# Rotary queries: four quarter-height ScalarE copies in place of a split and two permutation matmuls

## The chip, the cores and the metric

One core of a Trainium2 chip runs the whole program. The metric is the device time of one execution in microseconds (us); the times shown are of three executions of the kernel before.

## The reference, cut to what matters

The program is a two-layer decoder trunk over 1024 tokens of width 1024: an mLSTM layer, then a layer of latent attention, each with an MLP. The change lies in the attention layer's queries. Each of 8 heads has 128 plain and 64 rotary columns; the rotary ones are turned by the token's position:

```
def apply_rope(x, cos, sin):
    xf = x.astype(jnp.float32)
    x1, x2 = jnp.split(xf, 2, axis=-1)
    out = jnp.concatenate([x1 * cos - x2 * sin, x2 * cos + x1 * sin], axis=-1)
    return out.astype(x.dtype)
...
q = (cq @ w_q_b).reshape(B_, S, B_HEADS, B_NOPE + B_ROPE)
q_nope, q_rope = jnp.split(q, [B_NOPE], axis=-1)
q_rope = apply_rope(q_rope, cos[:, :, None, :], sin[:, :, None, :])
```

So a rotary query is x times cosines plus x with its two halves of 32 columns exchanged, times signed sines.

## The kernel before, in words

Activations lie transposed: features on the 128 partitions, 512 tokens (one half of the sequence) along the free axis. A float32 product is made of three TensorE matmuls: each operand is split into a rounded part hi (ScalarE copy, L499) and the rest lo (VectorE subtraction, L500), and `mm3` issues hi·hi, hi·lo and lo·hi (L280 to L282). Weights are split the same way after their DMA (L238 on ScalarE, L239 on VectorE).

The rotary queries of two heads (a "pair") fill one tile of 128 partitions: two heads times two halves of 32. Exchanging the halves therefore means that partitions 0-31 and 32-63 change places, and 64-95 and 96-127. This happens in `rope`, which is called for 4 pairs in each of the two halves of the sequence, 8 times in all. `rope` is a generator: the part ahead of its `yield` runs right behind the pair's matmuls, the part behind it some steps later. For the first half `rot` in `attention_first` calls it, for the second `prepare_pair` in `attention_second`; both hand the result to `query_rotary`, which splits it and writes the tile that the score matmuls read (L1762 on ScalarE, L1764 to L1767 on VectorE). I number the eight calls pair 1 to pair 8 in order of time.

The input of `rope`, `pt`, is a PSUM bank of the pool `pc` (two banks, shared with value projections, query projections and transposes of the softmax). The pools `ps` (two banks) and `pm` (two double banks) hold the dense work. `rope` takes tiles of the pool `tmc` (six).

Around it runs the dense work of an MLP: `two_streams` weaves the attention's steps with MLP steps, so that TensorE has matmuls of the MLP while the attention's vector work runs. Within that, a list scheduler with a timeline model of its own puts the instructions of each engine in an order when the program is built; a change of one step can so move others. Each engine runs its own list in order, and a wait holds all that stands behind it.

Names in the rows: `hd` is an MLP hidden tile (or a transposed softmax tile), `wk`, `wh`, `wl` are weights, `k` is a general 1024-column buffer, `tma` an accumulator of the adaLN vectors, `selW` the tile that holds the permutations. L980, L981 and L499 make a hidden tile's nonlinearity and its hi part on ScalarE, L500 on VectorE its lo part.

## Time and profile before

| | |
|---|---|
| time, median of 3 | 2322.63 us (2320.99 to 2323.7) |
| the profiled execution's own time | 2324.03 us |
| its span, first to last instruction | 2322.2 us |
| TensorE matmul busy | 2280.8 us (98%), 12042 matmuls |
| TensorE weight loads busy | 1921.8 us (83%) |
| VectorE busy | 1702.5 us (73%) |
| ScalarE busy | 1129.4 us (49%) |
| mean granted clock of TensorE | 0.998 |

Rows of a timeline give the start (us from the span's start), the duration, the engine, the line, the operation, output<-inputs and, in brackets, idle time ahead of it and who ended it. PE is TensorE's matmuls, DVE VectorE, ACT ScalarE. Matmuls and vector instructions overlap their successor's start, so the step from one start to the next is the price in a full queue, not the duration.

### The profile page before, as it was taken

How to read it: one execution, taken by the hardware profiler on the slowest of the kernel's cores; microseconds unless marked ns; L12 is line 12 of the kernel's file. 1: busy time of each engine (PE TensorE's matmuls, PEld its weight loads, DVE VectorE, ACT ScalarE, POOL GpSimd, SP SyncE). 2: the span in 40 equal slices, each digit the busy share in tenths (PEclk: the TensorE clock that was granted, in tenths of full speed). 3: DMA queues.
4: the chain of work that ended last, by engine and by line, in shares of the span. 5: the costliest groups of instructions: out<-in, count | busy, mean ns of one | idle time of the engine just before them, and what ended most of it. 6: DMA issues, size and time to landing. Idle time of an engine off the chain costs nothing.

```text
span 2322.2 us, 32704 instructions
## 1 busy us (share of the span) xinstructions
PE 2280.8 (98%) x12042; PEld 1921.8 (83%) x12042; DVE 1702.5 (73%) x2782; ACT 1129.4 (49%) x1919; POOL 90.7 (4%) x196
## 2 busy tenths in 40 slices
PE   8999999999999999999999999999999999999998
PEld 6888788888887877778888788888888888989997
DVE  6676776889887877677775687666666388788776
ACT  4364435765334445545444565434444454655443
POOL 1000000001022210000000000000000000000000
PEclk9999999999999999999999999999999999999999
DMA  9543454667999887666785654774334352445432
GB/s 320 173 129 118 134 176 153 196 220 267 330 276 295 277 283 275 191 192 203 238 256 186 226 199 145 252 236 151 129 99 149 115 168 82 146 149 173 128 109 109
DMA packets 401649, 444.38 MB, mean 191 GB/s; under 512 B 27123, under 2 KB 289328, under 8 KB 401488
## 3 DMA queue, kind: packets, MB, share of 16 engines
q1 hardware_dynamic: 388544, 397.09, 54.0%
q0 software_dynamic: 12944, 45.20, 5.2%
q8 instruction: 95, 1.56, 0.3%
q14 instruction: 66, 0.54, 0.1%
HBM read 343.65 MB, written 98.57 MB: 190 GB/s over the span
## 4 chain that ended last, share of the span: by engine, by line
PE 78%; DMA 8%; DVE 8%; issue 2%; ACT 2%; SPq 1%; POOL 0%; DVEq 0%; ACTq 0%; POOLq 0%
PE ps L280 13%; PE ps L282 13%; PE ps L281 13%; PE pm L280 8%; PE pm L281 8%; PE pm L282 8%; DMA raw<-in_mlp_w_dram 4%; PE pc L281 2%; PE pc L280 2%; PE pc L282 2%; DVE wl L239 1%; DVE k L247 1%; PE pc L1982 1%; DMA raw<-s 1%; PE pm L1787 1%
## 5 line engine op out<-in xcount | busy, mean ns | idle before, releaser
L238 ACT CAST wh<-raw 128x1024 fp32r<-128x1024 f32 (+2 forms) x317 | 321.4, 1016 | 430.5 <-PE ps L281 178.0
L239 DVE TENSOR_TENSOR wl<-raw,wh 128x1024 fp32r<-128x1024 f32 (+2 forms) x317 | 375.0, 1185 | 197.4 <-ACT wh L238 172.8
L280 PE MATMUL ps<-k,wh 128*128 128x512 f32 (+1 forms) x1252 | 476.4, 380 | 8.1 <-DVE u L247 1.6
L282 PE MATMUL ps<-k,wl 128*128 128x512 f32 (+1 forms) x1252 | 469.4, 375 | 0.5 <-DVE wl L239 0.5
L281 PE MATMUL ps<-k,wh 128*128 128x512 f32 (+1 forms) x1252 | 468.4, 374 | 0.0
L280 PEld LDWEIGHTS ps<-k,wh 128*128 128x128 f32 x1252 | 236.6, 189 | 55.0 <-issue 2.7
L282 PEld LDWEIGHTS ps<-k,wl 128*128 128x128 f32 x1252 | 236.3, 189 | 43.3 <-DVE wl L239 1.0
L281 PEld LDWEIGHTS ps<-k,wh 128*128 128x128 f32 x1252 | 236.6, 189 | 41.4 <-issue 1.4
L247 DVE TENSOR_TENSOR k<-k,pm 128x512 f32<-128x512 f32 (+1 forms) x250 | 192.3, 800 | 63.8 <-PE pm L282 63.2
L280 PE MATMUL pm<-wh,hd 128*128 128x512 f32 x488 | 193.5, 397 | 3.1 <-ACT raw L1793 1.8
L282 PE MATMUL pm<-wh,hd 128*128 128x512 f32 x488 | 190.5, 390 | 0.0
L281 PE MATMUL pm<-wl,hd 128*128 128x512 f32 x488 | 190.5, 390 | 0.0
L280 PEld LDWEIGHTS pm<-wh,hd 128*128 128x128 f32 x488 | 91.7, 188 | 24.8 <-ACT raw L1793 4.5
L282 PEld LDWEIGHTS pm<-wh,hd 128*128 128x128 f32 x488 | 91.7, 188 | 19.8 <-DVE hd L500 0.5
L281 PEld LDWEIGHTS pm<-wl,hd 128*128 128x128 f32 x488 | 91.8, 188 | 18.3 <-issue 0.5
L390 DVE SCALAR_TENSOR_TENSOR tma<-raw,cond,tma 128x512 f32<-128x512 f32 x120 | 89.5, 746 | 17.6 <-DMA raw<-in_ada_w_dram 8.4
L281 PE MATMUL pm<-hd,wk 128*128 128x512 f32 x256 | 100.1, 391 | 1.7 <-DVE hd L500 1.7
L1793 ACT ACTIVATE raw<-pm,sm 128x128 f32<-128x128 f32 (+3 forms) x64 | 47.5, 742 | 111.2 <-DVE sm L1792 107.6
L280 PE MATMUL pm<-hd,wk 128*128 128x512 f32 x256 | 100.9, 394 | 0.6 <-ACT hd L499 0.6
L280 PE MATMUL pm<-hd,wh 128*128 128x512 f32 x256 | 99.5, 390 | 1.1 <-ACT hd L499 0.8
L282 PE MATMUL pm<-hd,wl 128*128 128x512 f32 x256 | 99.9, 390 | 0.2 <-DVE wl L239 0.2
L281 PE MATMUL pm<-hd,wh 128*128 128x512 f32 x256 | 99.7, 390 | 0.2 <-DVE hd L500 0.2
(498 smaller groups left out, 4847.9 us busy)
## 6 DMA issues: line engine op xcount, KB each, us to landing
raw<-in_mlp_w_dram SPq DMA_DIRECT2D x176, 512.0 KB, 4.5
raw<-in_ada_w_dram SPq DMA_DIRECT2D x64, 512.0 KB, 4.6
raw<-in_mlp_w_dram SPq DMA_DIRECT2D x128, 256.0 KB, 4.7
raw<-in_a_w_in_dram SPq DMA_DIRECT2D x44, 512.0 KB, 4.3
lo<-wl POOLq DMA_DIRECT2D x32, 512.0 KB, 6.1
wk<-lo SPq DMA_DIRECT2D x64, 256.0 KB, 4.1
xs<-k SPq DMA_DIRECT2D x40, 256.0 KB, 4.5
raw<-in_a_w_out_dram SPq DMA_DIRECT2D x16, 512.0 KB, 4.8
```

What stands on the lines that cost most here:

```text
L238: nc.scalar.copy(hi[:, :n], r[:, :n])
L239: i = nc.vector.tensor_sub(lo[:, :n], r[:, :n], hi[:, :n].bitcast(F32))
L247: return f(*a, **k)
L280: nc.tensor.matmul(o, lh, rh, start=start, stop=False)
L281: nc.tensor.matmul(o, lh, rl, start=False, stop=False)
L282: pe_last[0] = nc.tensor.matmul(o, ll, rh, start=False, stop=stop)
L390: nc.vector.scalar_tensor_tensor(acc, r[kk], cond[:, k : k + 1], acc, ALU.mult, ALU.add)
L1787: nc.tensor.matmul(o[:, :w], qh, kh, start=False, stop=True)
L1793: nc.scalar.activation(pr[:, :n], f, AF.Exp, bias=m, scale=SCALE, accum_out=l)
L1982: nc.tensor.transpose(pt[:, ts(2 * e + i, P)], u.prs[i][:, ts(b + e, P)], ident)
```

## The change

`rope` no longer splits `pt` and no longer multiplies by a permutation. Four ScalarE copies of 32 partitions each read `pt` in PSUM and write the exchanged quarters to an SBUF tile; VectorE multiplies that tile by the sines in place. The permutation in `selW` is not built any more. The two other uses of the permutation idea (`both`, `both_perm`, for the key) stay.

```
-    perm = selW[:, 0]
...
-            nc.vector.tensor_copy(perm[:, s], ident[:, ts(q ^ 1, 32)])
...
     def rope(pt, hf):
 
-        hi, lo, t1 = tmc(F32R), tmc(F32R), tmc()
-        split_mod(hi, lo, pt, None)
+        t1, t2 = tmc(), tmc()
+        for q in range(4):
+            nc.scalar.copy(t2[ts(q, 32)], pt[ts(q ^ 1, 32)])
         nc.vector.tensor_mul(t1, pt, hf.cs[:, 0])
         yield
-        p2 = pc()
-        nc.tensor.matmul(p2, perm, lo, start=True, stop=False)
-        nc.tensor.matmul(p2, perm, hi, start=False, stop=True)
-        t2 = tmc()
-        nc.vector.tensor_mul(t2, p2, hf.cs[:, 1])
+        nc.vector.tensor_mul(t2, t2, hf.cs[:, 1])
         nc.vector.tensor_add(t1, t1, t2)
         return t1
```

In the changed program the copies are L1530, the two products L1531 and L1533 and the sum L1534 (before: L1532, L1538, L1539). Lines behind `rope` stand 5 lower: `query_rotary` is L1757 and L1759 to L1762, softmax L1786 to L1790.

The scheduler moves the rest. First place: VectorE around pair 2. Before (`tmc_9431` is pair 2's lo part, `tmc_9432` its product with the cosines, `hd_9450` the hidden tile):

```order
L239 TENSOR_TENSOR wl_9417<-raw_9413,wh_9416 128x640 [waits DMAHW5_49,DMAHW6_49,PE_49,Activation_49]
L1795 TENSOR_SCALAR raw_9385<-raw_9385,sm_9407 128x256 [waits DVE_49]
L247 TENSOR_TENSOR tmc_9124<-tmc_9124,ps_9436 128x512 [waits PE_49]
L500 TENSOR_TENSOR hd_9450<-tmc_9124,hd_9450 128x512 [waits Activation_49]
L366 TENSOR_REDUCE sm_9494<-pc_9489 128x4 [waits PE_49]
```

The same place now (`tmc_9424` is what the copies write, `hd_9444` the same hidden tile):

```order
L239 TENSOR_TENSOR wl_9410<-raw_9406,wh_9409 128x640 [waits DMAHW5_49,DMAHW6_49,PE_49,Activation_49]
L1531 TENSOR_TENSOR tmc_9423<-pc_9413,hd_8492 128x512 [waits Activation_49]
L1533 TENSOR_TENSOR tmc_9424<-tmc_9424,hd_8492 128x512
L247 TENSOR_TENSOR tmc_9117<-tmc_9117,ps_9430 128x512 [waits PE_49]
L1534 TENSOR_TENSOR tmc_9423<-tmc_9423,tmc_9424 128x512 [waits DVE_49]
L1759 COPY k_1650_9503<-tmp_9504 64x512 [waits Activation_49]
L1760 COPY k_1650_9503<-tmp_9504 64x512
L1761 TENSOR_TENSOR k_1650_9503<-tmc_9423,tmp_9504 64x512 [waits DVE_49]
L1762 TENSOR_TENSOR k_1650_9503<-tmc_9423,tmp_9504 64x512
L500 TENSOR_TENSOR hd_9444<-tmc_9117,hd_9444 128x512 [waits Activation_49]
L366 TENSOR_REDUCE sm_9488<-pc_9483 128x4 [waits PE_49]
```

The whole rest of `rope` and `query_rotary`, which stood behind the permutation matmuls, now stands ahead of the lo part of the hidden tile. The first product, L1531, waits for ScalarE, whose four copies read the same bank.

ScalarE at the same place now; before, one copy `tmc<-pc` of 128x512 stood first:

```order
L1530 COPY tmc_9424<-pc_9413 32x512 [waits PE_49]
L238 COPY wh_9409<-raw_9406 128x640 [waits DMAHW6_49,DMAHW5_49]
L1530 COPY tmc_9424<-pc_9413 32x512 x3
L1211 COPY wk_9450<-raw_9449 128x1024 [waits DMAHW7_49,DMAHW0_49,PE_49]
L980 ACTIVATE tmc_9117<-tmc_9117 128x512 [waits DVE_49]
L1757 COPY tmp_9504<-tmc_9423 128x512 [waits DVE_49]
L981 ACTIVATE tmc_9117<-tmc_9117 128x512 [waits Activation_49]
L499 COPY hd_9444<-tmc_9117 128x512 [waits Activation_49]
```

Three of the four copies stand behind a weight cast, and the first copy of `query_rotary` (L1757) has moved ahead of the hidden tile's last two steps.

Second place: TensorE at pair 2, where the hidden tile is read. Before:

```order
L364 MATMUL pc_9489<-ident,tma_9167 128x128 x4
L280 MATMUL pm_9463<-hd_9450,wk_9206 128x512
L281 MATMUL pm_9463<-hd_9450,wk_9206 128x512
L282 MATMUL pm_9463<-hd_9450,wk_9207 128x512
...
L1535 MATMUL pc_9507<-tmc_9431,selW 128x512
L1536 MATMUL pc_9507<-tmc_9430,selW 128x512
L280 MATMUL ps_9520<-hd_9368,k_1529_8851 128x256
```

Now:

```order
L364 MATMUL pc_9483<-ident,tma_9160 128x128 x4
L280 MATMUL pm_9457<-hd_9444,wk_9199 128x512
L281 MATMUL pm_9457<-hd_9444,wk_9199 128x512
L282 MATMUL pm_9457<-hd_9444,wk_9200 128x512
...
L280 MATMUL ps_9510<-hd_9361,k_1529_8847 128x256
```

The two matmuls with `selW` are gone; the readers of the hidden tile stand where they stood.

Third place: VectorE behind pair 3, at the keys of the next head (`k_1782` before, `k_1773` now). Before:

```order
L1539 TENSOR_TENSOR tmc_9995<-tmc_9995,tmc_10057 128x512 [waits DVE_49]
L500 TENSOR_TENSOR hd_10041<-u_1702_9747,hd_10041 128x512 [waits Activation_49]
L390 TENSOR_SCALAR tma_9912<-raw_10046,cond,tma_9912 128x512 [waits DMAHW0_49]
L500 TENSOR_TENSOR hd_10084<-pc_10085,hd_10083 128x512 [waits Activation_49]
L1764 COPY k_1766_10060<-tmp_10061 64x512 [waits Activation_49]
L1765 COPY k_1766_10060<-tmp_10061 64x512
L1766 TENSOR_TENSOR k_1766_10060<-tmc_9995,tmp_10061 64x512 [waits DVE_49]
L1767 TENSOR_TENSOR k_1766_10060<-tmc_9995,tmp_10061 64x512
L1791 TENSOR_REDUCE sm_10106<-pm_10092 128x1 [waits PE_49]
L390 TENSOR_SCALAR tma_9912<-raw_10046,cond,tma_9912 128x512 [waits DVE_49]
L500 TENSOR_TENSOR k_1782_10128<-ps_10130,k_1782_10128 128x512 [waits Activation_49]
```

Now:

```order
L1759 COPY k_1757_10047<-tmp_10048 64x512 [waits Activation_49]
L1760 COPY k_1757_10047<-tmp_10048 64x512
L1761 TENSOR_TENSOR k_1757_10047<-tmc_9983,tmp_10048 64x512 [waits DVE_49]
L1762 TENSOR_TENSOR k_1757_10047<-tmc_9983,tmp_10048 64x512
L1786 TENSOR_REDUCE sm_10093<-pm_10079 128x1 [waits PE_49]
L500 TENSOR_TENSOR hd_10032<-u_1696_9737,hd_10032 128x512 [waits Activation_49]
L390 TENSOR_SCALAR tma_9902<-raw_10037,cond,tma_9902 128x512 [waits DMAHW0_49]
L500 TENSOR_TENSOR hd_10071<-pc_10072,hd_10070 128x512 [waits Activation_49]
L1787 TENSOR_SCALAR sm_10093<-sm_10093 128x1 [waits DVE_49]
L500 TENSOR_TENSOR k_1773_10115<-ps_10117,k_1773_10115 128x512 [waits Activation_49]
```

`query_rotary` has moved from behind two other subtractions (`hd`) to ahead of them; between its end and the keys' subtraction stand other instructions than before.

## The prediction

> **What bounds the kernel now.** I read the page first: engine shares, the granted clock, the chain that ended last.

> ```profile
> PE 2280.8 (98%) x12042; PEld 1921.8 (83%) x12042; DVE 1702.5 (73%) x2782; ACT 1129.4 (49%) x1919; POOL 90.7 (4%) x196
> PEclk9999999999999999999999999999999999999999
> PE 78%; DMA 8%; DVE 8%; issue 2%; ACT 2%; SPq 1%; POOL 0%; DVEq 0%; ACTq 0%; POOLq 0%
> ```

> TensorE is busy for 98% of the span at full clock and holds most of the chain. Busy time alone does not say that its queue is full, since matmuls overlap. So I looked at the steps from one start to the next, in a timeline at the first of the eight places, and at its busy time by stretches around later ones.

> ```profile
> 978.49 0.39 PE L1535 MATMUL pc<-tmc,selW 128*128 128x512 f32 x1
> 978.72 0.39 PE L1536 MATMUL pc<-tmc,selW 128*128 128x512 f32 x1
> 978.95 0.39 PE L280 MATMUL pm<-hd,wk 128*128 128x512 f32 x1
> ```

> ```profile
> 1440.00:1460.00 20.00, 20.00 (x97) 16.89 (x97) 15.24 (x24) 8.28 (x13) 0.00 (x0) 1.00 0.86 288
> 1460.00:1480.00 20.00, 20.00 (x101) 16.98 (x100) 15.80 (x24) 9.26 (x16) 0.00 (x0) 1.00 0.77 241
> ```

> A 512-column matmul lasts 0.39 us but the next starts 0.23 us later (0.46 us for both permutation matmuls), with no gap between neighbours. In the stretches around pairs 5 and 6 (length, then PE, PEld, DVE, ACT busy) TensorE has no idle time, VectorE 4 to 5 us in 20, ScalarE more than half. A microsecond of matmuls taken away here is a microsecond of the end, unless a later engine makes TensorE wait.

> The table of waits over the stretch of the eight pairs shows how rare such waits are:

> ```profile
> PE pc L280 <- DVE hd L500: 2.0, 1, 2.0
> PE ps L280 <- DVE sm L1792: 0.8, 1, 0.8
> ```

> The first is ahead of pair 2 and not touched; the second comes behind pair 3 and is, below.

> **The change part by part.** The groups of the lines concerned:

> ```profile
> L499 ACT CAST tmc<-pc x8: 579/580/587, 970.8 to 1508.2; 128x512 fp32r<-128x512 f32 x8
> L500 DVE TENSOR_TENSOR tmc<-pc,tmc x8: 683/687/693, 971.4 to 1509.2; 128x512 fp32r<-128x512 f32 x8
> L1532 DVE TENSOR_TENSOR tmc<-pc,hd x8: 678/680/682, 972.0 to 1509.8; 128x512 f32<-128x512 f32 x8
> L1535 PE MATMUL pc<-tmc,selW x8: 389/390/396, 978.5 to 1522.5; 128*128 128x512 f32 x8
> L1536 PE MATMUL pc<-tmc,selW x8: 389/390/398, 978.7 to 1522.8; 128*128 128x512 f32 x8
> L1538 DVE TENSOR_TENSOR tmc<-pc,hd x8: 681/683/691, 979.1 to 1523.2; 128x512 f32<-128x512 f32 x8
> L1539 DVE TENSOR_TENSOR tmc<-tmc,tmc x8: 677/681/691, 980.4 to 1524.9; 128x512 f32<-128x512 f32 x8
> L1524 DVE CAST selW<-ident x4: 174/175/176, 266.8 to 267.0; 128x32 fp32r<-128x32 f32 x4
> ```

> *Removed on TensorE:* 16 matmuls, each a step of 0.227 us (0.46/2): **-3.6 us**, all on the path by the steps above.

> *Removed on VectorE:* 8 subtractions of 0.69 us and 4 copies of 0.175 us, 6.2 us in all. The product L1533 reads SBUF instead of PSUM; L1539 (two SBUF inputs, 0.681) and L1538 (one in PSUM, 0.683) cost the same. I cost this at nothing: VectorE has idle time at every pair, and where TensorE waits for it (pair 3), I count it there. The four copies of the permutation sat in the mLSTM stage; there the scheduler moves a few matmuls and VectorE steps past each other, none of which TensorE's full queue waits for as far as the order shows. I take 0, with 0.5 us either way, about one subtraction.

> *Added on ScalarE:* four copies of 32x512 for one of 128x512. The trace has none of 32 partitions; the nearest rows are the cast `tmc<-pc`, and one that works on 8 partitions:

> ```profile
> 970.78 0.58 ACT L499 CAST tmc<-pc 128x512 fp32r<-128x512 f32 x1
> 971.26 0.62 ACT L499 CAST hd<-tmc 128x512 fp32r<-128x512 f32 x1
> L707 ACT ACTIVATE tmc<-tmc 8x512 f32<-8x512 f32 x2 | 1.3, 632 | 4.2 <-DVE tmc L706 4.2
> ```

> 8 partitions take 0.63 us as 128 do (0.62): the columns cost, not the partitions. So a copy costs 0.58, with 0.48 us from start to start, and four end 3x0.48+0.58 = 2.02 us after the first start; ScalarE gains 8x3x0.48 = 11.5 us of work. Bounds for a copy: 0.15 us (a quarter, if partitions counted) and 1.06 us (0.58+0.48, if each waited for the one ahead to be written); I take 0.48, since the same engine, source and column count stand behind it.

> [...]

> *What is queued behind them.* The bank `pt` is free, and VectorE goes on, only when L1531 is through, and L1531 waits for ScalarE's copies. At pair 2:

> ```profile
> 1022.25 0.59 ACT L499 CAST tmc<-pc 128x512 fp32r<-128x512 f32 x1 [1.89 <-PE pc L282]
> 1023.19 0.73 ACT L238 CAST wh<-raw 128x640 fp32r<-128x640 f32 x1
> 1025.94 0.62 ACT L980 ACTIVATE tmc<-tmc 128x512 f32<-128x512 f32 x1
> 1027.26 0.62 ACT L499 CAST hd<-tmc 128x512 fp32r<-128x512 f32 x1
> 1024.15 0.81 DVE L239 TENSOR_TENSOR wl<-raw,wh 128x640 fp32r<-128x640 f32 x1
> 1025.13 0.68 DVE L247 TENSOR_TENSOR tmc<-tmc,ps 128x512 f32<-128x512 f32 x1
> 1027.91 0.69 DVE L500 TENSOR_TENSOR hd<-tmc,hd 128x512 fp32r<-128x512 f32 x1 [2.09 <-ACT hd L499]
> 1029.53 0.39 PE L281 MATMUL pm<-hd,wk 128*128 128x512 f32 x1
> 1084.91 0.41 DVE L1764 CAST k<-tmp 64x512 fp32r<-64x512 f32 x1
> 1087.08 0.54 DVE L1791 TENSOR_REDUCE sm<-pm 128x1 f32<-128x384 f32 x1
> ```

> The copies start at 1022.25 with the weight cast behind the first: 0.48+0.73+2x0.48+0.58 put the last end at 1025.0. L1531 and L1533 take steps of 0.60 (L500 at 971.4 to L1532 at 972.0), so L247 starts at 1026.2 instead of 1025.13, and L1534 ends at 1027.5. L980 follows L247 by 0.81, at 1027.0, so it doesn't hold `query_rotary`'s ScalarE copy, which runs 1027.5 to 1028.1. Its four VectorE steps take 2.17 (1084.91 to 1087.08), to 1030.3; only then comes the subtraction of `hd`, which ends at 1031.0. TensorE reads its result with L281 at 1029.53, which it would reach with a full queue: it waits **+1.5 us**. Bounds: 0 (if the subtraction is early enough after all: 0.93 us lay between its old end, 1028.60, and L281) and 2.5 us (the whole delay, 1030.3-1027.9, if that reserve is gone).

> [...] Could L1531 run beside the copies, the wait at pair 2 would be shorter by its step, 0.9 instead of 1.5 us.

> At pair 3 the wait by L1792 above lies here:

> ```profile
> 1087.92 0.39 PE L282 MATMUL ps<-k,wl 128*128 128x512 f32 x1
> 1089.06 0.50 PE L280 MATMUL ps<-k,wh 128*128 128x512 f32 x1 [0.76 <-DVE sm L1792]
> 1088.32 0.68 DVE L500 TENSOR_TENSOR k<-ps,k 128x512 fp32r<-128x512 f32 x1
> ```

> The step is 1.14 instead of 0.23 us: 0.91 lost. The bank wanted is that of the keys' subtraction at 1088.32, which ends just ahead. What sets that subtraction's start is the VectorE queue behind pair 3:

> ```profile
> 1074.89 0.59 ACT L499 CAST tmc<-pc 128x512 fp32r<-128x512 f32 x1 [2.84 <-PE pc L282]
> 1077.61 0.69 DVE L1083 TENSOR_TENSOR tmp<-tmp,ps 128x512 f32<-128x512 f32 x1
> 1087.66 0.75 DVE L390 SCALAR_TENSOR_TENSOR tma<-raw,cond,tma 128x512 f32<-128x512 f32 x1
> ```

> The copies, with a softmax step of 0.35 between them, end at 1077.3; L1531 and L1533 push L1083 from 1077.61 to 1078.5. From L1083 to the first hidden subtraction and past it is about 4.2 us as before, so `query_rotary` starts at 1082.7, not at 1084.91: it no longer stands behind the two other subtractions. Add its 2.17, the reduction (0.5), two subtractions (1.2), an L390 (0.66) and a small step: the keys' subtraction starts at 1087.3 and TensorE could go on at 1087.95. TensorE, 0.45 us of matmuls shorter, arrives at 1087.7 and waits 0.25: **-0.7 us**, bounds -0.9 and 0.

> At pairs 6 and 7 the second query projection takes `pt`'s bank. Pair 6:

> ```profile
> 1461.93 0.58 ACT L499 CAST tmc<-pc 128x512 fp32r<-128x512 f32 x1
> 1463.54 0.68 DVE L1532 TENSOR_TENSOR tmc<-pc,hd 128x512 f32<-128x512 f32 x1
> 1465.34 0.40 PE L280 MATMUL pc<-k,wh 128*128 128x512 f32 x1
> ```

> ScalarE now does three copies, a hidden cast (0.52 a step) and the fourth copy: its end is 1461.93+3x0.48+0.52+0.58 = 1464.5. VectorE, held by the hidden subtraction until 1464.65, runs L1531 to 1465.3: just in time for 1465.34. I take 0, bounds 0 and +0.4 us each. At pairs 1, 4, 5 and 8 the reader of what is delayed comes microseconds later; I take 0 with the same bounds for all four together.

> **Sum:** -3.6+1.5-0.7 = -2.8 us. From the profiled execution's 2324.03 that is 2321.2; its span is 2322.2, 1.8 us lie around it and stay. The median of the runs is 1.4 us lower, 2322.63, and I predict for it **2319.8 us** (-0.12%). A measurement of this kernel can tell about 0.2%, 4.65 us, from no change.

> **The rivals.** *All of the matmuls and more* (faster). The wait at pair 2 stays away and pair 3's goes wholly; VectorE's 6.2 us less also shorten one more wait of half a microsecond: -3.6-0.9-0.5 = -5.0, 2317.6 us. For it: the wait at pair 2 is the difference of a delay of 2.4 and a reserve of 0.9 us, both sums of many steps; against: the order there is plain. Chance 0.20.

> *Slow copies* (slower). If a copy that moves partitions costs c from start to start instead of 0.48, everything behind L1531 comes 4(c-0.48) later. At pairs 2, 6 and 7 there is no reserve, at pair 3 about 0.4 us. With c = 1.06 that is 2.3 us at four places less 0.4: +8.9, so +6.1 in all, 2328.7 us. It is slower than before from c = 0.67, and by over 0.2% from c = 0.97. Against it: `query_rotary`'s steps on VectorE that move 64 partitions take 0.69 like others; for it: no row has ScalarE writing to other partitions than it reads. Chance 0.13.

> *TensorE was not full.* If matmul steps could close up further, the 16 matmuls ran in gaps and their removal brings nothing, while the waits stay: +1.5-0.7 = +0.8, 2323.4 us. Against it: the even steps of 0.23 us around them. [...] Chance 0.05.

> **How the numbers follow.** The forecast has 0.62, and its own range from the bounds is -5.2 (-3.6-0.9-0.5-0.2) to +0.4 us. The range 2316.6 to 2325.0 adds a microsecond of spread between runs at the low end and, upward, reaches past the third rival and the forecast's bounds with 2 us of such spread; it leaves out the slow copies and the fastest cases. Faster by over 0.2% (below 2318.0) is most of the first rival and a corner of the forecast: 0.22. Slower by over 0.2% (above 2327.3) is the second rival and unforeseen order: 0.14. The rest, 0.64, is within.

> **What would show it.** Right: no L1535 and L1536 of before, four copies at 0.48 us steps, L1531 ending each time behind the fourth; a wait PE L281 <- DVE hd of 1 to 2 us at pair 2; the wait behind pair 3 near 0.2 us; the stretches at pairs 5 to 8 without idle time. Wrong: copies above 0.7 us apart, or a wait of over 1 us at pairs 6 and 7, or new waits in the mLSTM stage.

## The result, and the profile after

| | before | after |
|---|---|---|
| time, median of 16 executions each | 2320.05 us (2316.27 to 2324.54) | 2325.44 us (2320.30 to 2330.94) |
| ratio after to before, 95% interval | | 1.0027 (1.0020 to 1.0033) |
| the profiled execution's time and span | 2324.03, 2322.2 us | 2325.13, 2323.2 us |

The changed kernel is slower by 0.27%, 5.4 us between the medians. The forecast was 2.8 us faster than the 2322.63 us of the first three executions, 2319.8 us, with a range to 2325.0. From the page of the profile after: the busy line, the granted clock and the chain that ended last.

```profile
PE 2282.0 (98%) x12026; PEld 1923.1 (83%) x12026; DVE 1696.9 (73%) x2770; ACT 1144.5 (49%) x1943; POOL 90.7 (4%) x196
PEclk9999999999999999999999999999999999999999
PE 77%; DVE 9%; DMA 7%; issue 3%; ACT 3%; POOL 0%; SPq 0%; DVEq 0%; ACTq 0%; POOLq 0%
```

16 matmuls fewer, and TensorE's busy time is 1.2 us longer. The groups of the new lines (count, shortest/median/longest ns, first and last start):

```profile
L1530 ACT COPY tmc<-pc x32: 575/577/581, 968.0 to 1512.7; 32x512 f32<-32x512 f32 x32
L1531 DVE TENSOR_TENSOR tmc<-pc,hd x8: 683/690/692, 970.9 to 1513.3; 128x512 f32<-128x512 f32 x8
```

The first copy starts 2.8 us ahead of the cast that stood there before (970.8, in the prediction's rows). At the last pair the first copy, in the next row, starts 2.1 us behind its cast (1508.2); the 1512.7 above is that pair's fourth copy, behind another cast.

```profile
1510.27 1.76 ACT L1530 COPY tmc<-pc 32x512 f32<-32x512 f32 x3
```

Between pair 1 and pair 8 the new form loses 4.9 us, though 14 of the removed matmuls lie there. The lead at pair 1 is no gain of the change: the kernel before, run again, reached this cast at 966.9. The waits of TensorE around pairs 2 and 3 (1005 to 1110 us; total, count, longest):

```profile
PE pc L280 <- DVE hd L500: 2.0, 1, 2.0
PE ps L280 <- DVE sm L1789: 1.8, 1, 1.8
PE pm L281 <- DVE hd L500: 1.3, 1, 1.3
PE pm L280 <- ACT hd L499: 0.3, 1, 0.3
PE ps L280 <- DVE k L500: 0.2, 1, 0.2
```

The first is the old one ahead of pair 2. The third and fourth are pair 2's, new; the last is what is left of the 0.8 us behind pair 3. The second, behind pair 3, is new and was not foreseen. Pair 2 in the timeline of after:

```profile
1019.22 0.58 ACT L1530 COPY tmc<-pc 32x512 f32<-32x512 f32 x1
1020.45 1.76 ACT L1530 COPY tmc<-pc 32x512 f32<-32x512 f32 x3
1022.24 0.69 DVE L1531 TENSOR_TENSOR tmc<-pc,hd 128x512 f32<-128x512 f32 x1 [0.95 <-ACT tmc L1530]
1024.76 0.62 ACT L1757 CAST tmp<-tmc 128x512 fp32r<-128x512 f32 x1
1025.29 0.63 ACT L981 ACTIVATE tmc<-tmc 128x512 f32<-128x512 f32 x1
1025.41 0.42 DVE L1759 CAST k<-tmp 64x512 fp32r<-64x512 f32 x1 [0.69 <-ACT tmp L1757]
1026.98 0.69 DVE L1762 TENSOR_TENSOR k<-tmc,tmp 64x512 fp32r<-64x512 f32 x1
1027.70 0.69 DVE L500 TENSOR_TENSOR hd<-tmc,hd 128x512 fp32r<-128x512 f32 x1
1026.62 0.50 PE L280 MATMUL pm<-hd,wk 128*128 128x512 f32 x1 [0.29 <-ACT hd L499]
1028.44 0.50 PE L281 MATMUL pm<-hd,wk 128*128 128x512 f32 x1 [1.33 <-DVE hd L500]
```

It is the picture that the prediction drew: L1531 right behind the fourth copy, `query_rotary`'s four steps ahead of the hidden tile's subtraction, and TensorE's L281 waiting for that. Ahead of L280 the wait is for the hi part, since L1757 ran on ScalarE between L980 and L981. By steps L281 costs 1.6 us (1.82 from L280's start, 0.23 in a full queue) and L280 0.5. Behind pair 3, before and then after:

```profile
1092.12 0.69 DVE L1083 TENSOR_TENSOR tmp<-tmp,ps 128x512 f32<-128x512 f32 x1
1092.72 0.68 DVE L1084 TENSOR_TENSOR tmc<-tmc,ps 128x512 f32<-128x512 f32 x1
1093.32 0.68 DVE L239 TENSOR_TENSOR wl<-raw,wh 128x512 fp32r<-128x512 f32 x1
```

```profile
1093.18 0.62 ACT L238 CAST wh<-raw 128x512 fp32r<-128x512 f32 x1 [4.03 <-DMA raw<-in_kv_w_b_dram]
1093.83 0.69 DVE L239 TENSOR_TENSOR wl<-raw,wh 128x512 fp32r<-128x512 f32 x1 [2.36 <-ACT wh L238]
1095.10 0.68 DVE L1083 TENSOR_TENSOR tmp<-tmp,ps 128x512 f32<-128x512 f32 x1
1095.70 0.68 DVE L1084 TENSOR_TENSOR tmc<-tmc,ps 128x512 f32<-128x512 f32 x1
1094.15 0.60 PE L1896 MATMUL pc<-ident,raw 128*128 128x128 f32 x4
1096.53 0.36 PE L280 MATMUL ps<-hd,k 128*128 128x256 f32 x1 [1.77 <-DVE sm L1789]
```

L1083 and L1084 add a PSUM bank into SBUF, and TensorE needs that bank next. Before, they stood ahead of L239, the lo part of a value weight; now L239 stands ahead of them, its weight is still on its way, and VectorE sits idle for 2.36 us with the additions behind it. The releaser that the row names, L1789, only stands behind L1084 on VectorE. By steps it is 2.0 us here (2.38 from the transposes to L280, 0.35 before), 0.4 at the transposes that follow, less 0.6 of the old wait: +1.8.

At pairs 6 and 7 (pair 6 shown) the second query projection waits for the bank of `pt`, 0.5 us by steps each time:

```profile
1463.74 1.75 ACT L1530 COPY tmc<-pc 32x512 f32<-32x512 f32 x3
1465.52 0.62 ACT L499 CAST hd<-tmp 128x512 fp32r<-128x512 f32 x1
1466.17 0.58 ACT L1530 COPY tmc<-pc 32x512 f32<-32x512 f32 x1
1466.78 0.68 DVE L1531 TENSOR_TENSOR tmc<-pc,hd 128x512 f32<-128x512 f32 x1
1467.52 0.50 PE L280 MATMUL pc<-k,wh 128*128 128x512 f32 x1 [0.33 <-DVE tmc L1531]
```

And the waits have a price beyond themselves. Stretches of 3.41 us of after (length, busy times of PE, PEld, DVE, ACT, POOL, then the granted clock):

```profile
1012.67:1016.08 3.41, 1.43 (x9) 1.08 (x8) 3.37 (x8) 1.69 (x4) 0.00 (x0) 1.00 0.87 290
1016.08:1019.49 3.41, 3.41 (x10) 2.63 (x9) 2.05 (x8) 2.24 (x6) 0.00 (x0) 0.50 0.36 106
1026.32:1029.73 3.41, 1.79 (x8) 1.26 (x8) 2.96 (x6) 0.24 (x1) 0.00 (x0) 1.00 0.25 94
1029.73:1033.14 3.41, 3.41 (x18) 3.41 (x17) 2.37 (x3) 0.37 (x1) 0.00 (x0) 0.50 0.00 0
1094.59:1098.00 3.41, 1.40 (x11) 1.09 (x10) 2.95 (x6) 2.70 (x5) 0.20 (x1) 1.00 0.09 35
1098.00:1101.41 3.41, 3.41 (x19) 3.32 (x17) 0.98 (x2) 2.92 (x7) 0.00 (x0) 0.50 0.36 90
```

Each time a stretch in which TensorE was busy for only 1.4 to 1.8 us is followed by one at half clock (0.50), in which it does about half as much: 512-column matmuls step by 0.43 us from 1016.25 to 1019.23, by 0.23 from 1019.59 on. By an estimate from the granted 0.50 up to 1.7 us are lost. Before has only the first of these three (1015.13 to 1021.95):

```profile
1015.13:1018.54 3.41, 1.44 (x12) 1.22 (x11) 3.38 (x7) 2.20 (x5) 0.00 (x0) 1.00 0.94 322
1018.54:1021.95 3.41, 3.41 (x9) 2.64 (x9) 2.52 (x8) 1.40 (x3) 0.00 (x0) 0.50 0.55 155
```

The account between pair 1 and pair 8 of this profile: -3.2 us (14 matmuls of 0.227), +2.1 at pair 2, +1.8 behind pair 3, +1.0 at pairs 6 and 7, +3.4 for two more half-clock stretches: +5.1, against the 4.9 measured.

### The profile page after: what moved, and what is told of

Same layout as the page of the kernel before. It is cut to its first block, busy times and chain, and to the rows that moved or that the text cites. A ratio compares the mean times of both kernels' runs of the same rounds, so it can differ in the third digit from the quotient of the medians.

```text
span 2323.2 us, 32681 instructions
## 1 busy us (share of the span) xinstructions
PE 2282.0 (98%) x12026; PEld 1923.1 (83%) x12026; DVE 1696.9 (73%) x2770; ACT 1144.5 (49%) x1943; POOL 90.7 (4%) x196
## 4 chain that ended last, share of the span: by engine, by line
PE 77%; DVE 9%; DMA 7%; issue 3%; ACT 3%; POOL 0%; SPq 0%; DVEq 0%; ACTq 0%; POOLq 0%
PE ps L280 13%; PE ps L281 13%; PE ps L282 13%; PE pm L280 8%; PE pm L281 8%; PE pm L282 8%; DMA raw<-in_mlp_w_dram 4%; PE pc L280 1%; PE pc L281 1%; PE pc L282 1%; DVE k L247 1%; DVE wl L239 1%; PE pc L1977 1%; DVE hd L500 1%; PE pm L1782 1%
## 5 line engine op out<-in xcount | busy, mean ns | idle before, releaser
L238 ACT CAST wh<-raw 128x1024 fp32r<-128x1024 f32 (+2 forms) x317 | 321.3, 1016 | 424.8 <-PE ps L281 180.3
L239 DVE TENSOR_TENSOR wl<-raw,wh 128x1024 fp32r<-128x1024 f32 (+2 forms) x317 | 374.6, 1183 | 194.1 <-ACT wh L238 168.4
L280 PE MATMUL ps<-k,wh 128*128 128x512 f32 (+1 forms) x1252 | 476.1, 380 | 5.0 <-DVE tmc L1084 1.4
L282 PE MATMUL ps<-k,wl 128*128 128x512 f32 (+1 forms) x1252 | 468.9, 374 | 0.7 <-DVE wl L239 0.7
L281 PE MATMUL ps<-k,wh 128*128 128x512 f32 (+1 forms) x1252 | 468.3, 374 | 0.0
L280 PEld LDWEIGHTS ps<-k,wh 128*128 128x128 f32 x1252 | 236.4, 189 | 51.6 <-issue 2.6
L282 PEld LDWEIGHTS ps<-k,wl 128*128 128x128 f32 x1252 | 236.1, 189 | 43.3 <-DVE wl L239 1.1
L281 PEld LDWEIGHTS ps<-k,wh 128*128 128x128 f32 x1252 | 236.4, 189 | 41.2 <-issue 1.4
L247 DVE TENSOR_TENSOR k<-k,pm 128x512 f32<-128x512 f32 (+1 forms) x250 | 192.3, 801 | 70.6 <-PE pm L282 70.0
L280 PE MATMUL pm<-wh,hd 128*128 128x512 f32 x488 | 193.7, 397 | 2.5 <-ACT raw L1788 1.7
L282 PE MATMUL pm<-wh,hd 128*128 128x512 f32 x488 | 190.6, 391 | 0.0
L281 PE MATMUL pm<-wl,hd 128*128 128x512 f32 x488 | 190.6, 391 | 0.0
L280 PEld LDWEIGHTS pm<-wh,hd 128*128 128x128 f32 x488 | 91.7, 188 | 24.2 <-ACT raw L1788 4.3
L282 PEld LDWEIGHTS pm<-wh,hd 128*128 128x128 f32 x488 | 91.7, 188 | 19.8 <-DVE hd L500 0.5
L281 PEld LDWEIGHTS pm<-wl,hd 128*128 128x128 f32 x488 | 91.8, 188 | 18.3 <-issue 0.5
L281 PE MATMUL pm<-hd,wk 128*128 128x512 f32 x256 | 100.3, 392 | 3.0 <-DVE hd L500 3.0
L280 PE MATMUL pm<-hd,wk 128*128 128x512 f32 x256 | 101.0, 395 | 0.9 <-ACT hd L499 0.9
L280 PE MATMUL pm<-hd,wh 128*128 128x512 f32 x256 | 100.0, 393 | 1.6 <-ACT hd L499 1.6
L282 PE MATMUL pm<-hd,wl 128*128 128x512 f32 x256 | 100.6, 393 | 0.3 <-DVE wl L239 0.3
L500 DVE TENSOR_TENSOR hd<-tmp,hd 128x512 fp32r<-128x512 f32 x112 | 77.7, 696 | 31.6 <-ACT hd L499 31.2
L281 PE MATMUL pm<-hd,wh 128*128 128x512 f32 x256 | 100.2, 392 | 0.2 <-DVE hd L500 0.2
L390 DVE SCALAR_TENSOR_TENSOR tma<-raw,cond,tma 128x512 f32<-128x512 f32 x120 | 89.6, 747 | 14.7 <-DMA raw<-in_kv_ada_w_dram 7.6
```

What stands on the lines that cost most here:

```text
L238: nc.scalar.copy(hi[:, :n], r[:, :n])
L239: i = nc.vector.tensor_sub(lo[:, :n], r[:, :n], hi[:, :n].bitcast(F32))
L247: return f(*a, **k)
L280: nc.tensor.matmul(o, lh, rh, start=start, stop=False)
L281: nc.tensor.matmul(o, lh, rl, start=False, stop=False)
L282: pe_last[0] = nc.tensor.matmul(o, ll, rh, start=False, stop=stop)
```

## The experiments

My theory, *order*: what is lost is lost in VectorE's list, at pair 2 and behind pair 3, and in the half-clock stretches that waits of this size bring. Rivals: a *price per use*, the copies holding the bank and ScalarE wherever they stand; *chance*, clock and waits of single executions; and later, *not full*, matmuls that are not worth their step.

**Are clock and waits the change's own?** The kernel before and the changed one, run again.

> The kernel before once more, for its granted clock run by run. Two theories. Order: the new form's loss comes from waits of TensorE at two places (pair 2, and behind pair 3), each of about 2 us, and each able to bring a stretch of 3.41 us at half clock; then before, which has one such wait in this stage, shows a clock of 0.998 in most runs (one or two such stretches). Chance: the changed kernel's runs at 0.995 to 0.997 are drift of the chip; then before shows 0.997 and less as often. Ratio 1.000 within 0.001 by both.

Ratio 0.9996 (0.9988 to 1.0005). Mean clock 0.9981 over its 11 executions, and 0.9981 over the 35 of before on that chip; the changed kernel's 16 had 0.9969.

> The changed kernel once more, on the chip of the next three and with before's clock run by run. Order theory: a second profile shows the same two places (pair 2 and behind pair 3, 1.5 to 2.2 us each), and a mean clock about 0.001 under that of before; ratio 1.002 to 1.003. Chance: the two waits or the lower clock are of one run only; ratio near 1.001.

1.0031 (1.0019 to 1.0042), mean clock 0.9965 against 0.9977 for before on that chip. The profile shows the same places, the wait behind pair 3 again 1.8 us. Between pair 1 and pair 8 (TensorE's first L280 behind each pair's projection) it takes 542.9 us, and before, run again, 537.3: 5.7 us lost. This time no half clock followed the wait behind pair 3:

```profile
1096.00:1099.41 3.41, 1.63 (x10) 1.14 (x8) 2.63 (x6) 2.55 (x5) 0.20 (x1) 1.00 0.52 180
1099.41:1102.82 3.41, 3.13 (x25) 2.94 (x26) 1.93 (x4) 3.35 (x8) 0.00 (x0) 1.00 0.07 25
```

So the waits belong to the program; whether one is followed by half clock differs from execution to execution. In the mean the changed kernel's clock is 0.0012 lower, 2.8 us in 2320. Chance falls as the whole cause.

**Where is it lost?** The old form put back at some pairs, by a counter of `rope`'s calls:

```
     def rope(pt, hf):
+        if next(calls) not in (1, 3, 4, 5, 6, 7, 8):
+            hi, lo, t1 = tmc(F32R), tmc(F32R), tmc()
+            split_mod(hi, lo, pt, None)
...
```

The tuple leaves out pair 2 here, then pair 3, then both, then 2, 3, 6 and 7.

> The new form at all pairs but pair 2, where the old split and matmuls stand (the permutation is built). Order: the new waits at pair 2 (0.46 and 1.60 us) go, and with them a half-speed stretch (up to 1.7 us), two matmuls come back (0.45): 3.3 us under the changed kernel, ratio to before about 1.0013; the wait behind pair 3 (1.94 us) stays. Price per use (copies hold the bank and ScalarE wherever they stand; 6.3 us over eight uses): one eighth less, ratio 1.0024.

> The new form at all pairs but pair 3. Order: VectorE's list behind pair 3 is that of before again, so the weight's subtraction that waits for a transfer no longer stands ahead of the two additions that free TensorE's bank; the wait of 1.94 us goes, that of 0.92 us comes back, with a half-speed stretch and two matmuls 2.6 us under the changed kernel, ratio about 1.0016; pair 2's waits stay. Price per use: 1.0024.

> The new form at pairs 1 and 4 to 8, the old one at 2 and 3. Order: both losses go; 12 matmuls less (-2.7 us), 0.5 us of waits at each of pairs 6 and 7: -1.7 us, up to +0.4 if the two sums above simply add; ratio 0.9993 to 1.0002. Price per use: six eighths of the loss, 1.0020.

> The new form at pairs 1, 4, 5 and 8 only, where no row shows TensorE waiting behind it. By the step of 0.227 us a matmul: 8 matmuls, -1.8 us, ratio 0.9992, and 0.5 to 1 us below the kernel that has it also at 6 and 7, where 1 us of waits stands against 0.9 us of matmuls: about equal to it. If matmuls taken away there only open gaps (TensorE not full): 1.000.

| old form at pair | ratio to before | mean clock (before's) |
|---|---|---|
| 2 | 1.0008 (0.9999 to 1.0016) | 0.9973 (0.9981) |
| 3 | 1.0016 (1.0008 to 1.0025) | 0.9968 (0.9981) |
| 2, 3 | 1.0005 (0.9996 to 1.0014) | 0.9977 (0.9981) |
| 2, 3, 6, 7 | 1.0000 (0.9990 to 1.0010) | 0.9978 (0.9980) |

The first two waits come and go with their pair, one row from the kernel with pair 2 old, and two from the one with pair 3 old (1005 to 1110 us):

```profile
PE ps L280 <- DVE sm L1805: 1.9, 1, 1.9
```

```profile
PE pm L280 <- ACT hd L499: 1.5, 1, 1.5
PE pm L281 <- DVE hd L500: 1.3, 1, 1.3
```

With both pairs old neither is left, and the ratio falls to where a price per use (1.0020) is outside the interval. The last two ratios lie above what *order* forecast (1.0002 at most, and 0.9992), the second where *not full* put it; the intervals don't exclude the forecasts. Each pair's order is its own cause: old at 3 puts L239 behind the two additions again, whatever stands at 2.

**Is it the order, or that VectorE is late?** All pairs new, one edge of order added. For pair 2:

```
+        with tc.issue_after(lasts[0]) if next(nq) in (2,) else nullcontext():
             nc.vector.tensor_copy(T[0:64, 0], hi[0:64].bitcast(F32))
...
```

`lasts[0]` is the last hidden tile's subtraction; `next(nq)` counts the calls of `query_rotary`.

> The changed kernel, with one edge of order more: at pair 2 query_rotary's four VectorE steps stand behind the hidden tile's subtraction, not ahead of it. All eight pairs keep the new form. Order theory: the wait PE L281 <- DVE hd (1.3 to 1.6 us) at pair 2 shrinks to 0.3 or less, with the half-clock stretch that it can bring, while the two matmuls stay away: 2 to 3.5 us under the changed kernel, ratio to before 1.0012 to 1.0018; the wait behind pair 3 stays. Rival (the copies that hold pt's bank delay everything at pair 2, whatever stands behind them): the wait stays over 1 us, ratio 1.0024 or more.

1.0021 (1.0010 to 1.0031), mean clock 0.9975 (0.9980). The 1.6 us of waits at pair 2 are 0.4:

```profile
PE pm L282 <- DVE hd L984: 0.2, 1, 0.2
PE pm L281 <- ACT hd L983: 0.2, 1, 0.2
```

The wait is the order's; the gain in time (1.0027 to 1.0021) is less than forecast and inside the intervals, and the wait behind pair 3 is 2.2 us in this profile. For pair 3, the value weights split in a later step of the generator, alone and with the edge at pair 2:

```
+            w = (prompt(wdma) if p_ == 2 else wload)(vw, 256)
             yield
+            if p_ == 2:
+                with tc.issue_after(adds[0]):
+                    w = prompt(wfin)(*w)
```

`wdma` issues the transfer, `wfin` the cast and the subtraction; `adds[0]` is the last L1084.

> The changed kernel, with the value weights of one head pair split later: their VectorE subtraction, which waits for a transfer behind pair 3, stands behind the two additions that free TensorE's bank. All eight pairs keep the new form. Order theory: the wait PE ps <- DVE (1.8 us) behind pair 3 goes, without another of its size unless the value products then wait for these weights; 1.5 to 3 us under the changed kernel, ratio 1.0014 to 1.0021. Rival (VectorE is simply late there since the copies came late): the wait stays over 1 us, ratio 1.0024 or more.

> The two edges of order together, the new form at all eight pairs. Order theory: both losses go and all 16 matmuls stay away: the sum of the single effects, 3.5 to 6 us under the changed kernel, ratio 1.000 to 1.0012, and a mean clock like that of before (0.998). It would be under before (0.9990) only if pairs 6 and 7 cost nothing. Rival: 1.0022 or more.

1.0060 (1.0045 to 1.0075) and 1.0053 (1.0036 to 1.0070): both forecasts missed. The 1.8 us are gone, but the ScalarE cast went with the subtraction, and the value products wait for it (the first of the two):

```profile
PE pc L287 <- ACT wh L239: 7.4, 1, 7.4
```

So only the subtraction was moved, to right behind the two additions:

```
                     nc.vector.tensor_add(u3, u3, pt)
-                    nc.vector.tensor_add(u2, u2, pt)
+                    i = nc.vector.tensor_add(u2, u2, pt)
+                    with tc.issue_after(i.ins):
+                        while late_lo:
+                            late_lo.pop()()
```

`late_lo` holds that one subtraction.

> The changed kernel, with only the VectorE subtraction of those value weights held back: it is issued right behind the two additions that free TensorE's bank (the ScalarE cast stays early, unlike in the kernel that split them late). All eight pairs new. Order theory: the wait PE ps <- DVE (1.8 us) behind pair 3 goes, and no 7 us wait for the weights comes in its place; 1 to 3 us under the changed kernel, ratio 1.0012 to 1.002. Rival (VectorE is late there whatever its list): the wait stays over 1 us.

1.0015 (1.0007 to 1.0024), against 1.0031 for the unchanged order on the same chip. From 1080 to 1110 us one wait is left:

```profile
PE ps L293 <- DVE k L513: 0.3, 1, 0.3
```

> This edge and the one at pair 2 together, new form at all eight pairs. Order theory: waits as in before save 0.5 us at each of pairs 6 and 7, so -3.6+1.0+0.4 (rest at pair 2) -0.6 (the wait behind pair 3 that was 0.9) = -2.8 us, ratio 0.9988, clock as before. If the loss had a third source spread over the pairs: 1.001 or more.

> The same with the old form at pairs 6 and 7: 12 matmuls less, no wait at 6 and 7: -2.7+0.4-0.6 = -2.9 us, ratio 0.9987; the best that the order theory has to offer. With a third source at each use: six eighths of what the kernel with all eight shows.

1.0003 (0.9994 to 1.0012), and with the old form at 6 and 7 0.9999 (0.9990 to 1.0007); mean clocks 0.9975 and 0.9977 (0.9977). Two edges, which take no instruction away, bring back nearly all of the loss: order is shown for that part. But the forecasts of 0.9988 and 0.9987 lie outside the intervals: the 2.8 us gain didn't come, and something takes the 16 matmuls' 3.6 us.

**Is the bank the third source, or are the matmuls worth nothing?** One copy more, of 0.58 us, frees `pt`'s bank ahead of the other four:

```
+            nc.scalar.copy(t1, pt)
             for q in range(4):
-                nc.scalar.copy(t2[ts(q, 32)], pt[ts(q ^ 1, 32)])
-            nc.vector.tensor_mul(t1, pt, hf.cs[:, 0])
+                nc.scalar.copy(t2[ts(q, 32)], t1[ts(q ^ 1, 32)])
+            nc.vector.tensor_mul(t1, t1, hf.cs[:, 0])
```

> The new form with one ScalarE copy more: all of pt is copied to SBUF first (0.58 us), the four quarters are then taken from that copy, and the product with the cosines reads it too. So pt's bank is free one copy after it is full, not after four copies and a VectorE step, and in the program's list the two additions and the value weights' subtraction behind pair 3 stand as before; at pair 2 query_rotary still stands ahead of the hidden tile's subtraction. Bank theory (what is left of the loss beside pairs 2 and 3 is the bank held at pairs 6 and 7): no PE pc <- DVE wait at pairs 6 and 7, none of 1.8 us behind pair 3; the pair 2 wait stays (1.5 to 2.5 us, and clock): ratio 0.9995 to 1.001. Not-full theory (matmuls taken away here are not worth their step): 1.001 to 1.002.

> The same with the edge of order at pair 2 (query_rotary behind the hidden tile's subtraction). Bank theory: all three sources gone, 16 matmuls saved: -3.6 to -2.5 us, ratio 0.9984 to 0.9990, the first kernel under before. Not-full theory: 1.000 to 1.0005, as the kernel with both edges of order showed.

> The kernel before, with the two permutation matmuls of each pair issued five times over into the same bank (each time from a fresh start, so the result is the same): 64 matmuls more, nothing else. Full theory: 64 times 0.227 us = +14.5 us, ratio 1.0063. Not-full theory: VectorE and ScalarE catch up while TensorE works on them, waits elsewhere shrink, and a matmul costs half its step or less: 1.003 or less.

64 matmuls more cost 13.5 us by the ratio, 1.0058 (1.0044 to 1.0073): 0.21 us each (0.16 to 0.26), the step of 0.227. This interval alone leaves room for some 4 us of gaps that the first matmuls could fill; the profiles are closer. The stretch from pair 1 to pair 8 in before, and with 56 of the 64 in it (columns as in the stretches above; x counts instructions):

```profile
969.63:1507.40 537.77, 528.20 (x2561) 439.08 (x2559) 390.19 (x646) 261.62 (x443) 4.16 (x24) 1.00 0.67 214
967.38:1517.08 549.70, 541.18 (x2617) 449.31 (x2615) 391.88 (x646) 261.93 (x443) 4.03 (x24) 1.00 0.65 210
```

It is 11.9 us longer, the waits listed in it are 8.4 us in place of 9.5, and each has one half-clock stretch: 13.0 us for 56 matmuls, 0.23 each. "Not full" falls: TensorE's queue has no room there. The bank theory is not borne out whole either. Five copies give 1.0014 (1.0003 to 1.0025), and with the edge at pair 2 1.0006 (0.9997 to 1.0014), where 0.9990 at most was forecast; both are close to what "not full" forecast, though that theory has lost its ground. From 1430 to 1530 us, pairs 5 to 8, no wait of TensorE is left (0.7 us by the table in after): the bank was the source of those waits at pairs 6 and 7. But at pair 2 the longer row of copies makes ScalarE late with the hidden tile (with the edge, 1016 to 1110 us):

```profile
PE pm L281 <- ACT hd L983: 1.9, 1, 1.9
```

**Without any of the three.** Five copies at pairs 5 to 8 and the old form at 1 to 4; and the same with four copies from PSUM at 1 and 4.

> Five copies (the whole bank first) in the second half, pairs 5 to 8, where the kernel with five copies everywhere showed no wait at pairs 6 and 7; the old split and matmuls at pairs 1 to 4. Bank theory: 8 matmuls less, no new wait: -1.8 us, ratio 0.9992, interval touching 1. If ScalarE's 5 x 0.48 us a pair delays something else there: 1.000 or more.

> The same, and four copies straight from PSUM at pairs 1 and 4 too, where nothing waits behind them; the old form at pairs 2 and 3 alone. Order and bank theory together: 12 matmuls less, no new wait: -2.7 us, ratio 0.9988, below before beyond the interval if it is right. If the loss has still another source: 1.000.

Both 0.9991 (0.9982 to 0.9999), medians 2318.01 and 2319.15 against 2320.82 us. These are the first below before, by 0.09%; the interval just excludes 1, and both are set against the same executions of before. Pairs 1 and 4 (0.9 us) are too small to be told apart here. The stretch from pair 1 to pair 8 agrees. Ten of the second kernel's 12 removed matmuls lie in it, 2.3 us (the row has 11 fewer than before; the one more is not explained):

```profile
967.10:1503.25 536.15, 526.42 (x2550) 436.87 (x2549) 387.97 (x641) 272.43 (x461) 4.17 (x24) 1.00 0.66 212
```

It is 1.1 to 1.6 us shorter than in two profiles of before (537.3 and 537.8), and the waits listed in it are 9.6 us, 0.1 to 1.0 more.

## Why the prediction was wrong

- *The matmuls, -3.6 us:* right as far as the runs tell; 64 more of them cost 0.21 us each, 0.23 by the profiles.
- *The copies:* each lasts 0.58 us as said, but they step by 0.59 (three in 1.76 us: 1.76-0.58 over two), not 0.48: between copies ScalarE overlapped nothing, while two casts of 128 partitions did, by 0.10 (the rows 970.78 and 971.26).
- *Pair 2, +1.5:* the mechanism, the instructions and the waiting line are as forecast; +2.1 by steps, of which 0.5 is the wait for the hi part on ScalarE. I had asked whether L980 delays `query_rotary`'s copy (L1757), not what that copy, ahead of L981 and L499, does to the hi part.
- *Behind pair 3, -0.7:* **the step that failed.** The wait that I worked on went as forecast (0.8 to 0.2 us). I followed VectorE's list up to the keys' subtraction and stopped; eight instructions further L239 had moved ahead of L1083 and L1084, and the weight that it needs comes by a transfer. In place of -0.7 stands +1.8. Orders of this kind were in the prediction only as the "unforeseen order" in the chance of 0.14.
- *Pairs 6 and 7, 0 (up to +0.4 each):* +0.5 each; "just in time" was right with the steps that I took. From the first copy to the fourth it is 2.43 us (1463.74 to 1466.17) in place of 1.96: 0.11 for each of three steps, and 0.13 for the hidden cast between them.
- *mLSTM stage, 0:* no loss there. From 200 to 955 us TensorE's listed waits are 7.8 and 7.9 us in two profiles of after, 9.2 and 6.1 in two of before.
- *The rivals:* the copies were slower than priced, but far from the step of 1.06 us of that rival; "TensorE was not full" fell with the 64 matmuls; "all of the matmuls and more" needed pair 2 without a wait.
- *The signs of being wrong:* none of the three was seen. The copies are 0.59 us apart, pairs 6 and 7 wait 0.5 us each, and the mLSTM stage shows no more waiting than before. None of the signs covered what stands further down a list.
- *Slips:* the upper bounds, as written, add to +0.6, not +0.4 us. And the two waits that I called rare are 2.8 us of the 11.1 that the table lists in that stretch.
- *Not in the sum at all:* the clock, **a term left out without a reason.** A mean clock lower by 0.0012 is 2.8 us, on top of the waits that cause it.

The sum with the measured terms is -3.6+2.1+1.8+1.0 = +1.3, with the clock +4.1, against +5.4 between the medians and +4.6 to +7.7 by the interval of the ratio. Of the 8.2 us between forecast and medians the clock is thus 2.8, pair 3 2.5, pairs 6 and 7 1.0, pair 2 0.6, and 1.3 are left. Of this rest, one part shows: waits at the same places differ between executions (PE pm L280 <- ACT hd 0.3 us at pair 2 in one profile of the changed kernel, 1.4 in the other). With both edges of order the waits of the stage add up to 12.7 us by the table, against 11.1 and 10.2 in two profiles of before; 0.7 of that is the bank. Between pair 1 and pair 8 its profile takes 539.5 us, 1.7 to 2.3 more than the two of before. The 14 matmuls are -3.2, the listed waits (11.1 against 9.5 and 8.6) +1.6 to +2.5, and one half-clock stretch more +1.7; 1.2 to 1.6 us stay open. A wait cost 0.2 to 0.3 us more by steps than the table gives (0.5 for 0.33, 1.6 for 1.33, 2.0 for 1.77), and there are 15 in place of 9 and 11, so by an estimate from these differences 0.7 to 1.6 us of the rest are waits too. The third source is then small waits scattered over the stage, and the clock; no run tests this. Why the scheduler put L239 ahead at pair 3 is argued only: its timeline expects the weight earlier than it came.

## What to carry to other kernels

A few matmuls of a full queue were worth their step here (64 more cost 0.21 to 0.23 us each), and no more; a vector instruction that changes its place cost 2 us here, nine matmuls. When a change moves an engine's list, walk it until it is the old one again, and at each place ask of every instruction that now stands in front whether it waits for something slow, a transfer above all (VectorE sat idle for 2.36 us by one here). Compare several executions: two single profiles here differed by 1.0 us in span, and the kernels by 5.4.

## What the runs showed of the hardware

| TensorE busy in the step, us | the next step |
|---|---|
| 1.02, 1.46 (after_again), 1.40, 1.43 (after), 1.43 (evac58), 1.44 (before), 1.47, 1.50 (old2) | 0.50, 8 of 8 |
| 1.61 (mix), 1.62 (behind2), 1.73 (evac58), 1.75 (control), 1.79 (after) | 0.50 |
| 1.63 (after_again), 1.77 (before) | 1.00 |
| 1.84, 1.87 (behind2), 1.90 (after) and all above | 1.00 |

The steps that half clock followed thus held 1.6 to 2.4 us without a matmul (3.41 less 1.79 and 1.02). So by an estimate from these rows a wait of 2 us cost 2 us or 3.7 (1.7 for a step at 0.50), by how it lay to these steps: the wait of 1.8 us behind pair 3 was followed by 0.50 in after (1.40 us busy) and not in after_again (1.63).

ScalarE copies of 32 partitions, back to back, did not overlap here: four from an SBUF tile (the kernel with five copies) take 2.50 us, a step of 0.63, and each lasts 0.62. From PSUM it was 0.59 and 0.58. A copy from PSUM that moves 32 partitions to another quarter (0.577) thus took what a cast of all 128 took in place (0.580).

```profile
1459.79 2.50 ACT L1531 COPY tmc<-tmc 32x512 f32<-32x512 f32 x4
```
